# Opening stage of a hybrid encoder block: order of VectorE's work, sums of squares in pairs on GpSimd, row sums without a split

## The chip, the cores and the metric

The kernel runs on one core of a Trainium2 chip. A core has five engines that run side by side, each with its own queue, in order: TensorE (matmuls, into PSUM), VectorE, ScalarE, GpSimd and SyncE, which issues most DMAs. The profile calls them PE (and PEld for the loading of weights), DVE, ACT, POOL and SP. They share the on-chip memory SBUF and wait for each other through semaphores. The metric is the device time of one execution in microseconds (us); lower is better.

## The reference

The block takes 1024 positions of width 1024, puts 16 learned meta tokens in front (1040 positions), normalizes, projects into ten parts, runs a bidirectional retention and a windowed attention on them, merges, projects and normalizes again. What matters here is the start: the norm, the projection, and q, k and v of retention head 0.

```python
def _rms_norm(x, w):
    xf = x.astype(jnp.float32)
    y = xf * lax.rsqrt(jnp.mean(xf * xf, axis=-1, keepdims=True) + EPS)
    return (y * w.astype(jnp.float32)).astype(x.dtype)

def _hybrid_layer(h, pre_w, w_in, dec_f, dec_b, ...):
    u = _rms_norm(h, pre_w)
    z = u @ w_in
    rq, rk, rv, rg, aq, ak, av, ag, gr, ga = _split_in(z)
    rq = _pad_front(_rotary(rq.reshape(B, T, RET_HEADS, RET_DK), pos))
    rk = _pad_front(_rotary(rk.reshape(B, T, RET_HEADS, RET_DK), pos) * (RET_DK ** -0.5))
    rv = _pad_front(rv.reshape(B, T, RET_HEADS, RET_DV).astype(jnp.float32))
    lg_f = jax.nn.log_sigmoid(dec_f.astype(jnp.float32))
    lg_b = jax.nn.log_sigmoid(dec_b.astype(jnp.float32))
    o_r = _bidirectional_retention(rq, rk, rv, lg_f, lg_b)[:, META_PAD:]
    ...
```

The decays are powers of `exp(lg)`. The norm's factor of a row is a scalar, so the kernel projects `x * w` first and applies the factor later.

## The kernel before

**Precision.** Every operand of a large product is split into a high part (rounded to the fast matmul type, `R` in the code) and a low part (the rest), and a product is three matmuls: high times high (L74), then the two mixed ones (L75, L76). High parts are made by ScalarE or GpSimd, low parts by VectorE (`dve_lo`, L90, a subtraction; for x L329, one instruction that scales and subtracts).

**The opening stage.** x lies transposed, in eight blocks `xr[k]` of 128 channels by 1040 positions, loaded in order. For each block k:

- ScalarE makes the high part `xh[k]` (L327) and then the squares `sq[k]` (L348);
- VectorE makes the low part `xl[k]` (L329). In the trace both parts are called `big`;
- TensorE multiplies the block with the weights `w0` of q and k of head 0 into six PSUM banks (`qk0_mm`, L310; tiles `pq`, `pk`): first the products with the high part of x, last those with the low part (L76).

The weights w0 come in pieces; the low parts of the third piece (`third`, blocks 2 and 3) and of the last (`fifth`, blocks 4 to 7; in the trace `w<-wr`) are VectorE's too. Beside this stands a chain of small instructions on 8 columns, the decays: `exponentials`, `decays`, `decay_series` (nine steps that each need the one before), `decay_exponents`, and on GpSimd a power for the table `dtab` (`decay_columns`, L236).

The squares are summed block after block on VectorE (`add_square`, L321). The sum is then split, high on ScalarE (L361) and low on VectorE (`sql`), and TensorE multiplies both parts with a column of ones, 128 positions at a time, which gives the mean square of each row (`sums_by_rows`, L370, tile `pms`). These small products stand between those of the third V product.

**Behind the blocks** come: `pack_meta` (L151, the 16 meta columns of each block into `xm`); the weights of V, cast by ScalarE (L115, `wh`) and their low parts on VectorE (`wl`); three V products on TensorE (`projT`, tile `pv`): first that of the meta rows (L159, L161), then those of 128 rows each. The second and third need a PSUM bank that a piece of qk0 still holds. `evac_qk0(i)` frees it: VectorE rotates piece i by three multiplications from PSUM (L184 to L186, tile `m_qk`) and GpSimd adds two of the results (L187).

**What sets the order.** Each engine runs its queue in order. The queue is fixed when the program is built: a scheduler places the instructions by its estimate of when each can run, and `issue_after(i)` holds an instruction behind instruction i. Before the change the holds put on VectorE: low part 2, the whole decay chain up to the exponents, the first add of squares, and only then low part 3; from block 4 on the low part of block k stands behind the add of sums[k - 2]; and all adds but the last split stand before the first rotation.

## Time and profile before

| What | Value |
|---|---|
| Median of 3 runs | 1075.31 us (1073.83 to 1077.41) |
| The profiled execution | 1075.24 us |
| Its span, first to last instruction | 1073.5 us |
| Busy share: PE, PEld | 98%, 84% |
| Busy share: DVE, ACT, POOL | 81%, 45%, 20% |

A row of a timeline has start, duration, engine, source line, operation, tiles (written `<-` read), shapes, a count where equal rows are merged (the duration is then that of all), and in brackets how long the engine was idle before it and what ended that. A row of the waits has who waited for whom, us in total, how many times, and the longest. A row of groups has busy time, mean ns of one, and the idle time before. Source lines that name a helper stand for all its callers, so L90 is any low part but that of x, and L187 any add of a rotation.

### The profile page before, as it was taken

Reading aid. Unit: us, or ns where it says so; the run is one execution under the profiler, and the core shown is the slowest. Engines: PE = TensorE matmul, PEld = TensorE weight load, DVE = VectorE, ACT = ScalarE, POOL = GpSimd, SP = SyncE. Lnnn points to the kernel's source line nnn. Section 1 sums busy time; section 2 is a strip of 40 time slices with the busy share of each in tenths; the row PEclk is TensorE's granted clock in tenths of the full one; section 3 lists DMA queues with packets and bytes.
Section 4 is the critical chain, followed back from the end, with each engine's and each line's share of the span. In section 5 each row is a group of like instructions: output and inputs, shape, how many; then the busy total and the mean of one; then the engine's idle time right before and its main releaser. Section 6 shows DMA issues by size and latency. Waiting matters only on the chain.

```text
span 1073.5 us, 17195 instructions
## 1 busy us (share of the span) xinstructions
PE 1049.6 (98%) x5863; PEld 905.7 (84%) x5863; DVE 867.9 (81%) x1770; ACT 487.0 (45%) x1064; POOL 217.2 (20%) x270
## 2 busy tenths in 40 slices
PE   8999999999999999989999999999999999999997
PEld 7898999989989788878888888888888888787886
DVE  7897788768986677787668988999799799767765
ACT  7141442422413444456557545555456546333432
POOL 3234225133352333342210000000000000110032
PEclk9999999999999999999999999999999999999999
DMA  7121111203131455576758769899934746789464
GB/s 285 40 70 43 57 41 60 84 28 102 51 108 49 140 178 178 166 241 223 220 169 272 265 232 313 275 360 345 377 129 157 241 172 221 234 206 326 122 118 78
DMA packets 109304, 187.14 MB, mean 174 GB/s; under 512 B 10864, under 2 KB 49648, under 8 KB 108400
## 3 DMA queue, kind: packets, MB, share of 16 engines
q1 hardware_dynamic: 105328, 179.47, 50.5%
q0 software_dynamic: 3456, 6.29, 3.9%
q8 instruction: 46, 0.75, 0.3%
q10 hardware_dynamic: 432, 0.28, 0.1%
q14 instruction: 42, 0.34, 0.1%
HBM read 124.92 MB, written 61.87 MB: 174 GB/s over the span
## 4 chain that ended last, share of the span: by engine, by line
PE 86%; DVE 6%; DMA 3%; issue 2%; ACT 2%; POOL 1%; SPq 0%; DVEq 0%; POOLq 0%; ACTq 0%
PE bz L75 8%; PE bz L74 8%; PE bz L76 8%; PE pv L74 3%; PE pv L75 3%; PE pv L76 3%; PE paq L75 3%; PE paq L76 3%; PE paq L74 3%; PE br L75 2%; PE br L74 2%; PE br L76 2%; PE bo L75 2%; PE bo L74 2%; PE bo L76 2%; PE ba L75 2%
## 5 line engine op out<-in xcount | busy, mean ns | idle before, releaser
L1210 POOL DMA_DIRECT2D mx_d<-c1a x4 | 3.7, 918 | 396.2 <-DVE c1a L1201 396.2
L75 PE MATMUL bz<-T,llz 128*128 128x512 f32 x192 | 75.7, 394 | 0.0
L76 PE MATMUL bz<-T,lhz 128*128 128x512 f32 x192 | 75.6, 395 | 0.0
L74 PE MATMUL bz<-T,lhz 128*128 128x512 f32 x192 | 75.4, 394 | 0.0
L74 PE MATMUL pv<-wh,big 128*128 128x256 f32 x256 | 73.2, 286 | 1.3 <-DVE m_qk L186 1.3
L75 PE MATMUL pv<-wh,big 128*128 128x256 f32 x256 | 73.2, 286 | 0.0
L76 PE MATMUL pv<-wl,big 128*128 128x256 f32 x256 | 72.5, 283 | 0.0
L75 PE MATMUL bz<-big,llz 128*128 128x512 f32 x176 | 69.7, 396 | 0.0
L76 PE MATMUL bz<-big,lhz 128*128 128x512 f32 x176 | 69.3, 394 | 0.0
L74 PE MATMUL bz<-big,lhz 128*128 128x512 f32 x176 | 68.6, 394 | 0.0
L1379 POOL TENSOR_SCALAR p<-p,den 128x352 f32<-128x352 f32 (+2 forms) x60 | 44.6, 757 | 92.7 <-DVE den L1372 88.4
L1369 ACT ACTIVATE p<-raw,nm 128x353 f32<-128x353 f32 (+2 forms) x64 | 36.0, 565 | 47.7 <-DVE nm L1366 46.8
L74 PE MATMUL paq<-big,wh 128*128 128x512 f32 x128 | 51.4, 402 | 0.0
L75 PE MATMUL paq<-big,wl 128*128 128x512 f32 x128 | 50.6, 396 | 0.0
L76 PE MATMUL paq<-big,wh 128*128 128x512 f32 x128 | 50.5, 394 | 0.0
L74 PEld LDWEIGHTS pv<-wh,big 128*128 128x128 f32 x256 | 48.3, 189 | 1.7 <-DVE m_qk L186 1.6
L75 PEld LDWEIGHTS pv<-wh,big 128*128 128x128 f32 x256 | 48.3, 189 | 0.2
L76 PEld LDWEIGHTS pv<-wl,big 128*128 128x128 f32 x256 | 48.3, 189 | 0.0
L1366 DVE CUSTOM_DVE_ANT_0 raw<-ps,mask,nsink 128x352 f32<-128x352 f32 (+2 forms) x64 | 33.4, 553 | 16.1 <-PE ps L76 15.8
L75 PEld LDWEIGHTS bz<-T,llz 128*128 128x128 f32 x192 | 36.2, 188 | 8.5
L74 PEld LDWEIGHTS bz<-T,lhz 128*128 128x128 f32 x192 | 36.2, 188 | 8.4
L76 PEld LDWEIGHTS bz<-T,lhz 128*128 128x128 f32 x192 | 36.2, 188 | 8.4
(620 smaller groups left out, 3574.4 us busy)
## 6 DMA issues: line engine op xcount, KB each, us to landing
wrz<-in_w_in_dram SPq DMA_DIRECT2D x32, 512.0 KB, 5.7
wr<-in_w_in_dram SPq DMA_DIRECT2D x31, 512.0 KB, 4.0
e<-e SPq DMA_DIRECT2D x40, 256.0 KB, 4.5
we<-in_w_in_dram SPq DMA_DIRECT2D x16, 512.0 KB, 5.2
tg<-tg_d SPq DMA_DIRECT2D x32, 256.0 KB, 5.1
T<-preT SPq DMA_DIRECT2D x6, 1024.0 KB, 7.1
oTr_d<-ost SPq DMA_DIRECT2D x16, 256.0 KB, 2.1
aq_d<-aq SPq DMA_DIRECT2D x16, 256.0 KB, 2.2
```

The costliest lines, as they stand in the source:

```text
L74: nc.tensor.matmul(o, ah, bh, start=first, stop=False, **kw)
L75: nc.tensor.matmul(o, al, bh, start=False, stop=False, **kw)
L76: latest[:] = [nc.tensor.matmul(o, ah, bl, start=False, stop=last, **kw).ins]
L1210: nc.gpsimd.dma_start(d, to, accum_op=ALU.add)
L1366: nc.vector.tensor_tensor_reduce(raw[e_][:, 1:1 + wid], s[:, 0:wid], mask[:, mo:mo + wid], -SCALE, nsink[:, hp:hp + 1], ALU.add, ALU.min, ...
L1369: last["exp"] = nc.scalar.activation(p[:, 0:1 + wid], raw[e_][:, 0:1 + wid], AF.Exp, scale=-1.0, bias=nm_[:, e_:e_ + 1], accum_out=den[:, ...
L1379: nc.gpsimd.tensor_scalar(pt[e_][:, 0:wid], pt[e_][:, 0:wid], den[:, e_:e_ + 1], 1.0, op0=ALU.mult, op1=ALU.mult)
```

## The change

It concerns the opening alone:

- VectorE makes each block's low part before other work for that block; the decay chain is cut into pieces that stand behind the low parts of blocks 2 to 5.
- Squares are added in pairs (0 and 1, 2 and 3, 4 and 5, 6 and 7) on GpSimd; VectorE adds the four pair sums with three adds, one before block 6, one behind V's low parts, one behind the first rotation.
- The row sums take the sum of squares as plain float32: no split, one product in place of two.
- The low parts of V's weights are held behind the packing of the meta rows, one after the other (`"apart"` returns them for that), and six buffers for squares replace four.

```diff
@@ -115,9 +115,11 @@
                 nc.scalar.copy(h, t)
             else:
                 pool_hi(h, t)
-            dve_lo(l, t, h)
             hi.append(h)
             lo.append(l)
+            if act == "apart":
+                return lambda: dve_lo(l, t, h)
+            dve_lo(l, t, h)
 
         return split, ((lambda k, a, b: hi[k // 4][:, k % 4, a:b]), (lambda k, a, b: lo[k // 4][:, k % 4, a:b]))
 
@@ -192,7 +194,7 @@
     tabt = ra.tile([P, MW], F32, tag="tab", bufs=1, name="tabt")
     idx = tabt[:, 3 * P:3 * P + 5]
     warm = ra.tile([P, 1], F32, name="warm")
-    ones, onef = (ra.tile([P, 2], t, name=n) for n, t in (("ones", R), ("onef", F32)))
+    onef = ra.tile([P, 2], F32, name="onef")
     dect, neg, na, e, e2, s_, ss, acc, lg = (ra.tile([P, 8], F32, name=n) for n in (
         "dect", "neg", "na", "e", "e2", "s_", "ss", "acc", "lg"))
     ecst, ex = (ra.tile([P, 28], F32, name=n) for n in ("ecst", "ex"))
@@ -217,12 +219,13 @@
         v.tensor_tensor(ss, s_, s_, ALU.mult)
         v.tensor_scalar(acc, ss, 1.0 / 17, None, op0=ALU.mult)
 
-    def decay_series():
+    def decay_series(first, last):
         v = nc.vector
-        for j in (15, 13, 11, 9, 7, 5, 3):
-            v.scalar_tensor_tensor(acc, acc, 1.0 / j, ss, op0=ALU.add, op1=ALU.mult)
-        v.scalar_tensor_tensor(acc, acc, 1.0, s_, op0=ALU.add, op1=ALU.mult)
-        v.scalar_tensor_tensor(lg, acc, -2.0, lg, op0=ALU.mult, op1=ALU.add)
+        for j in (15, 13, 11, 9, 7, 5, 3, 1)[first:last]:
+            v.scalar_tensor_tensor(acc, acc, 1.0 / j, ss if j > 1 else s_, op0=ALU.add, op1=ALU.mult)
+
+    def decay_log():
+        nc.vector.scalar_tensor_tensor(lg, acc, -2.0, lg, op0=ALU.mult, op1=ALU.add)
 
     def decay_exponents():
         v = nc.vector
@@ -313,61 +316,68 @@
                     k == 0, k == KT - 1)
 
         nc.vector.memset(onef, 1.0)
-        nc.vector.tensor_copy(ones, onef)
         nc.vector.memset(ms, 1.0)
-        low, squares, sums = None, [], {}
-
-        def add_square(k):
-            sums[k] = nc.vector.tensor_tensor(squares[k], squares[k - 1], squares[k], ALU.add).ins
+        squares, at = [], [None]
+
+        def then(f):
+            with follow(*[x for x in at if x is not None]):
+                r = f()
+            if r is not None:
+                at[:] = [r if hasattr(r, "name") else r.ins]
+
+        def low(k, a, b):
+            return nc.vector.scalar_tensor_tensor(xl[k][:, a:b], xr[k][:, a:b], vec[:, k:k + 1],
+                                                  xh[k][:, a:b].bitcast(F32), op0=ALU.mult, op1=ALU.subtract)
+
+        def add_squares(e, i, k):
+            return e.tensor_tensor(squares[k], squares[i], squares[k], ALU.add)
 
         for k in range(KT):
             t = xr[k]
-            parts = [(0, 528), (528, T)] if k == 0 else [(0, T)]
-            for a, b in parts:
+            for a, b in [(0, 528), (528, T)] if k == 0 else [(0, T)]:
                 nc.scalar.activation(xh[k][:, a:b], t[:, a:b], AF.Copy, scale=vec[:, k:k + 1])
-                with tc.issue_after(sums[k - 2] if k > 3 else exponents) if k > 2 else ExitStack():
-                    low = nc.vector.scalar_tensor_tensor(xl[k][:, a:b], t[:, a:b], vec[:, k:k + 1],
-                                                         xh[k][:, a:b].bitcast(F32), op0=ALU.mult, op1=ALU.subtract)
+                then(lambda: low(k, a, b))
+            if k == 0:
+                with tc.issue_after(raised[1]):
+                    then(exponentials)
+                nc.gpsimd.tensor_tensor(e, ecst[:, 0:8], na, ALU.pow)
+            if k == 1:
+                then(third)
             if k == 2:
-                with tc.issue_after(low.ins):
-                    decays()
-                    decay_series()
-                    exponents = decay_exponents()
+                then(decays)
+            if k == 3:
+                then(lambda: decay_series(0, 3))
+                then(fifth)
+            if k == 4:
+                then(lambda: decay_series(3, 6))
+            if k == 5:
+                then(lambda: decay_series(6, 8))
+                then(decay_log)
+                then(decay_exponents)
+            qk0_mm(k)
+            squares.append(st.tile([P, T], F32, tag="sq", bufs=6, name=f"sq{k}"))
+            nc.scalar.activation(squares[k], t, AF.Square)
+            if k % 2:
+                add_squares(nc.gpsimd, k - 1, k)
+            if k == 5:
                 decay_columns()
-            if k == 0:
-                with tc.issue_after(low.ins), tc.issue_after(raised[1]):
-                    exponentials()
-                    nc.gpsimd.tensor_tensor(e, ecst[:, 0:8], na, ALU.pow)
-            if k == 1:
-                third()
-            if k == 3:
-                with tc.issue_after(exponents):
-                    fifth()
-            qk0_mm(k)
-            squares.append(st.tile([P, T], F32, tag="sq", bufs=4, name=f"sq{k}"))
-            nc.scalar.activation(squares[k], t, AF.Square)
-            if k > 1:
-                with tc.issue_after(exponents if k == 2 else low.ins):
-                    add_square(k - 1)
-        with tc.issue_after(low.ins):
-            pack_meta()
-            wv0 = load_w(w_in, U_V, act=True)
-
-        add_square(KT - 1)
-        with tc.issue_after(sums[KT - 1]):
-            rotated = evac_qk0(0)
-        sq = squares[-1]
-        sqh, sql = (st.tile([P, T], R, name=n) for n in ("sqh", "sql"))
-        nc.scalar.copy(sqh, sq)
-        with tc.issue_after(rotated):
-            split = dve_lo(sql, sq, sqh)
+                then(lambda: add_squares(nc.vector, 1, 3))
+        raw_v = fetch_w(w_in, U_V)
+        split_v, wv0 = halves_w(U_V)
+        then(pack_meta)
+        for t in raw_v:
+            then(split_v(t, "apart"))
+        then(lambda: add_squares(nc.vector, 3, 5))
+        rotated = evac_qk0(0)
+        at[:] = [rotated]
+        then(lambda: add_squares(nc.vector, 5, 7))
+        split, sq = at[0], squares[-1]
         pms = p1("pms")
 
         def sums_by_rows(k):
             for c in (k, 8)[:1 + k // 7]:
                 a, b = cols(c)
-                for i, t in enumerate((sqh, sql)):
-                    nc.tensor.matmul(pms[0:b - a, 2 * c:2 * c + 2], t[:, a:b], ones, start=i == 0, stop=i == 1)
+                nc.tensor.matmul(pms[0:b - a, 2 * c:2 * c + 2], sq[:, a:b], onef, start=True, stop=True)
 
         with tc.issue_after(split):
             rotated = evac_qk0(1)
```

ScalarE now takes each block's squares right behind its high part and casts V's weights last; TensorE's products of blocks 4 to 7 interleave a little differently; SyncE's queue is the same, and behind the opening all queues are the same as before. Three places in the queues follow; a row is line, operation, tiles (with numbers of the program's own), shape and, where rows are merged, a count.

GpSimd (POOL) from the high part of the third piece of w0 (`w0_0_0`) to the first adds of a rotation (`kr0`, `qr0`), before:

```order
L87 TENSOR_SCALAR w0_0_0_154<-wr0_0_153 128x512
L236 TENSOR_TENSOR dtab_103<-ecst_135,ex_136 128x28
L187 TENSOR_TENSOR kr0_429<-m1_qk0_0_430,m2_qk0_0_431 128x272
L187 TENSOR_TENSOR kr0_429<-m1_qk0_1_441,m2_qk0_1_442 128x256
L187 TENSOR_TENSOR qr0_4_536<-m1_qk0_4_537,m2_qk0_4_538 128x512
```

and now:

```order
L87 TENSOR_SCALAR w0_0_0_153<-wr0_0_152 128x512
L333 TENSOR_TENSOR sq1_251<-sq0_228,sq1_251 128x1040
L333 TENSOR_TENSOR sq3_305<-sq2_279,sq3_305 128x1040
L333 TENSOR_TENSOR sq5_359<-sq4_331,sq5_359 128x1040
L239 TENSOR_TENSOR dtab_103<-ecst_134,ex_135 128x28
L333 TENSOR_TENSOR sq7_406<-sq6_384,sq7_406 128x1040
L189 TENSOR_TENSOR kr0_426<-m1_qk0_0_427,m2_qk0_0_428 128x272
```

Three adds of squares now stand between the weight's high part and the power for dtab, and one between that and the first rotation.

VectorE (DVE) from the end of the decay chain to the low part of block 5 (`xr5`) before; `big` with `xr` is a low part of x, `w0_1_1` the low part of the last piece of w0:

```order
L229 TENSOR_TENSOR ex_136<-lg_134,tabt_122 128x16
L232 TENSOR_SCALAR ex_136<-lg_134,tabt_122 128x4
L233 TENSOR_SCALAR ex_136<-lg_134 128x8
L321 TENSOR_TENSOR sq1_253<-sq0_230,sq1_253 128x1040
L329 SCALAR_TENSOR_TENSOR big0_1_111<-xr3_148,vec_100,big0_0_109 128x1040
L90 TENSOR_TENSOR w0_1_1_158<-wr0_1_156,w0_1_0_157 128x1024
L321 TENSOR_TENSOR sq2_293<-sq1_253,sq2_293 128x1040
L329 SCALAR_TENSOR_TENSOR big1_1_112<-xr4_149,vec_100,big1_0_110 128x1040
L321 TENSOR_TENSOR sq3_317<-sq2_293,sq3_317 128x1040
L329 SCALAR_TENSOR_TENSOR big1_1_112<-xr5_150,vec_100,big1_0_110 128x1040
```

and now, from the last of the decay steps that stand behind block 2 to the first behind block 5:

```order
L219 TENSOR_TENSOR ss_131<-s__130 128x8
L329 SCALAR_TENSOR_TENSOR big0_1_111<-xr3_147,vec_100,big0_0_109 128x1040
L220 TENSOR_SCALAR acc_132<-ss_131 128x8
L225 SCALAR_TENSOR_TENSOR acc_132<-acc_132,ss_131 128x8 x2
L90 TENSOR_TENSOR w0_1_1_157<-wr0_1_155,w0_1_0_156 128x1024
L225 SCALAR_TENSOR_TENSOR acc_132<-acc_132,ss_131 128x8
L329 SCALAR_TENSOR_TENSOR big1_1_112<-xr4_148,vec_100,big1_0_110 128x1040
L225 SCALAR_TENSOR_TENSOR acc_132<-acc_132,ss_131 128x8 x3
L329 SCALAR_TENSOR_TENSOR big1_1_112<-xr5_149,vec_100,big1_0_110 128x1040
L225 SCALAR_TENSOR_TENSOR acc_132<-acc_132,ss_131 128x8
```

The adds of squares are gone from between the low parts, and steps of the series stand there.

VectorE around the low parts of V's weights (`wl4`) and the first rotation (`m1_qk0_0`, `m2_qk0_0`), before:

```order
L90 TENSOR_TENSOR wl4_0_421<-wr4_0_416,wh4_0_420 128x1024
L90 TENSOR_TENSOR wl4_1_425<-wr4_1_417,wh4_1_424 128x1024
L321 TENSOR_TENSOR sq6_386<-sq5_363,sq6_386 128x1040
L151 CAST xm_113<-big1_1_112 128x4x16
L321 TENSOR_TENSOR sq7_409<-sq6_386,sq7_409 128x1040
L184 TENSOR_TENSOR m1_qk0_0_430<-pk0_0_194,cr_119 128x272
L185 TENSOR_TENSOR m2_qk0_0_431<-pk0_0_194,sr_120 64x272
L186 TENSOR_TENSOR m2_qk0_0_431<-pk0_0_194,sr_120 64x272
L164 TENSOR_TENSOR vmeta0_447<-pv0_0_448,vmeta0_447 16x256
```

and now:

```order
L153 CAST xm_113<-big1_1_112 128x4x16
L90 TENSOR_TENSOR wl4_0_418<-wr4_0_409,wh4_0_417 128x1024
L90 TENSOR_TENSOR wl4_1_422<-wr4_1_410,wh4_1_421 128x1024
L333 TENSOR_TENSOR sq5_359<-sq3_305,sq5_359 128x1040
L186 TENSOR_TENSOR m1_qk0_0_427<-pk0_0_193,cr_119 128x272
L187 TENSOR_TENSOR m2_qk0_0_428<-pk0_0_193,sr_120 64x272
L188 TENSOR_TENSOR m2_qk0_0_428<-pk0_0_193,sr_120 64x272
L333 TENSOR_TENSOR sq7_406<-sq5_359,sq7_406 128x1040
```

One add of squares stands ahead of the rotation instead of two, and one behind it; the sum of the meta rows (`vmeta0`) has moved further back.

## The prediction

> **What bounds the kernel now.** I read the table of busy shares first (TensorE 98%, VectorE 81%), then TensorE's waits over the whole span, to see where the missing 2% lies.
>
> ```profile
> engine line waited for: us in total, times, longest us
> ...
> PE pt L1390 <- DVE pal L90: 2.3, 1, 2.3
> PE pq L76 <- DVE big L329: 2.0, 2, 1.6
> ...
> PE pv L74 <- DVE m_qk L186: 1.3, 1, 1.3
> PE pv L159 <- DVE xm L151: 0.9, 1, 0.9
> ```
>
> Three of these four are in the opening: L329 makes the low part of an x block, L151 packs the meta rows, L186 ends the first rotation. Together 2.0 + 1.3 + 0.9 = 4.2 us, and each releaser is VectorE. Next the opening by stages (length, then busy time of PE, PEld, DVE, ACT, POOL).
>
> ```profile
> 17.30:36.50 19.20, 15.00 (x96) 12.80 (x94) 19.10 (x26) 10.26 (x11) 5.20 (x1) 1.00 0.47 167
> 36.50:45.00 8.50, 8.48 (x73) 8.46 (x74) 5.80 (x12) 1.23 (x4) 3.77 (x5) 1.00 0.02 5
> ```
>
> From 17.3 to 36.5 VectorE is full (19.10 of 19.20) and TensorE has 4.2 us of holes; from 36.5 on TensorE is full. So one place decides: the start of the second V product at 36.52, which waits for a bank that the rotation of qk0 piece 0 frees.
>
> ```profile
> 36.02 0.44 DVE L186 TENSOR_TENSOR m_qk<-pk,sr 64x272 f32<-64x272 f32 x1
> 36.52 0.39 PE L74 MATMUL pv<-wh,big 128*128 128x256 f32 x1 [1.29 <-DVE m_qk L186]
> ```
>
> VectorE ends that rotation at 36.46 and TensorE starts 0.06 later. Behind it both programs have the same order on TensorE except the row sums, and no wait that a DMA ends is in the list, so whatever moves 36.52 moves the end by as much. The profiled execution took 1075.24 us, 1.74 over its span of 1073.5; the median of the runs shown is 1075.31, 0.07 above.
>
> **The change part by part.** *Fewer adds on VectorE.* Its queue had seven adds of squares ahead of the rotation; it keeps two there (sq3 += sq1, sq5 += sq3) and one behind it.
>
> ```profile
> L321 DVE TENSOR_TENSOR sq<-sq,sq 128x1040 f32<-128x1040 f32 x7 | 8.6, 1234 | 0.0
> 16.59 1.23 DVE L321 TENSOR_TENSOR sq<-sq,sq 128x1040 f32<-128x1040 f32 x1
> 17.74 1.29 DVE L329 SCALAR_TENSOR_TENSOR big<-xr,vec,big 128x1040 fp32r<-128x1040 f32 x1
> ```
>
> An add holds the queue for 17.74 - 16.59 = 1.15 us, so five fewer give 5.75 us. The decay series keeps its instructions, now between the low parts; low part 3 no longer stands behind 13 of them and an add, which is the 1.6 us hole.
>
> *Four adds on GpSimd.* The trace has no add of 1040 columns there; the nearest are the rotation's adds.
>
> ```profile
> L187 POOL TENSOR_TENSOR qr<-m_qk,m_qk 128x512 f32<-128x512 f32 x2 | 2.6, 1282 | 3.8 <-DVE m_qk L186 3.8
> L187 POOL TENSOR_TENSOR kr<-m_qk,m_qk 128x256 f32<-128x256 f32 x3 | 2.3, 750 | 5.4 <-DVE m_qk L186 5.4
> ```
>
> (1282 - 750) / 256 = 2.08 ns a column, so 1282 + 528 x 2.08 = 2.38 us each. Were they beside VectorE's work they would cost nothing. The trace says they are not beside it:
>
> ```profile
> 240.78 0.40 POOL L87 TENSOR_SCALAR Shb<-Sb 128x256 fp32r<-128x256 f32 x1
> 241.15 1.04 POOL L87 TENSOR_SCALAR wh<-wr 128x1024 fp32r<-128x1024 f32 x1
> 241.21 1.25 DVE L90 TENSOR_TENSOR Slb<-Sb,Shb 128x256 fp32r<-128x256 f32 x1 [0.89 <-POOL Shb L87]
> 447.75 1.47 POOL L187 TENSOR_TENSOR aq<-m_aq,m_aq 128x512 f32<-128x512 f32 x1 [3.38 <-issue]
> 447.99 2.31 DVE L90 TENSOR_TENSOR wl<-wr,wh 128x1024 fp32r<-128x1024 f32 x1
> 67.53 1.21 DVE L90 TENSOR_TENSOR wl<-wr,wh 128x1024 fp32r<-128x1024 f32 x1
> 67.60 1.40 POOL L87 TENSOR_SCALAR Shf<-Sf 128x256 fp32r<-128x256 f32 x1 [1.84 <-DVE klf L502]
> 69.40 0.41 DVE L90 TENSOR_TENSOR Slf<-Sf,Shf 128x256 fp32r<-128x256 f32 x1
> ```
>
> A VectorE subtraction of 256 columns takes 0.41; that at 241.21 took 1.25 and ended at 242.46, 0.27 after GpSimd's 241.15 + 1.04. One of 1024 columns takes 1.21; that at 447.99 took 2.31 and ended 1.08 after GpSimd's add. Both ended later than GpSimd by just their own columns (1.05 ns each): they did no work until GpSimd was done. At 67.60 it is the other way: GpSimd's copy, 0.40 alone, began in effect at 69.00 - 0.40 = 68.60, which is 0.14 before the recorded end of VectorE's subtraction. So instructions of the two engines take turns, whole, when VectorE reads two tiles from SBUF. In this opening nearly all do: low parts, weight low parts, adds, the series.
>
> The Trainium skill ("SBUF — State Buffer", section "Who interferes with whom") has this as an exclusive lock on a port pair against any GpSimd instruction that reads SBUF, held for the whole instruction. There the trace disagrees in one place, the power for dtab:
>
> ```profile
> 16.76 5.74 POOL L236 TENSOR_TENSOR dtab<-ecst,ex 128x28 f32<-128x28 f32 x1 [5.41 <-DVE ex L233]
> ```
>
> VectorE's low part at 17.74 ran its usual 1.29 within it. By the page taken literally the power, now among the adds, would add up to 5.7 us; by the row nothing, and I count nothing.
>
> *The turns, one by one.* ScalarE sets when each add can start:
>
> ```profile
> 14.11 1.06 ACT L348 ACTIVATE sq<-xr 128x1040 f32<-128x1040 f32 x1
> 16.00 3.27 ACT L327 ACTIVATE big<-xr,vec 128x1040 fp32r<-128x1040 f32 x3
> 10.35 1.00 POOL L87 TENSOR_SCALAR w<-wr 128x512 fp32r<-128x512 f32 x1
> 11.38 0.69 DVE L90 TENSOR_TENSOR w<-wr,w 128x512 fp32r<-128x512 f32 x1 [0.51 <-POOL w L87]
> 12.22 1.30 DVE L329 SCALAR_TENSOR_TENSOR big<-xr,vec,big 128x1040 fp32r<-128x1040 f32 x1
> ```
>
> First: sq1 is long ready when GpSimd ends its weight copy at 11.35, so its add starts at once (as at 240.78 + 0.40 and 241.15), ahead of VectorE's 11.38. It ends near 13.70, the weight's low part at 13.70 + 0.54 = 14.24 instead of 12.07. VectorE stood until 12.22 then anyway, so low part 2 starts 1.95 later, at 14.17.
> Second: sq3 is ready at 15.17; the add takes over 0.14 before low part 2 ends (15.47), so 15.33 to 17.71. The first small decay instruction ends at 17.73 instead of 15.60: +2.15.
> Third: ScalarE now alternates high parts and squares from 16.00 (1.06 and 0.96 apart), sq5 is ready at 20.14. The weight's low part (20.2 to 21.4) goes first, the add 21.25 to 23.63, and the next decay step is 2.15 late. If the add wins there, the weight pays the same.
> Fourth: the exponents end near 27.8, the power 33.6, the add follows V's second low part (34.56): 34.4 to 36.8. VectorE's sq5 += sq3 is queued just there, and with it the rotation: +2.2.
> Sum on VectorE's queue: 1.95 + 2.15 + 2.15 + 2.2 = 8.45, less 5.75: **+2.7 us**. The rotation ends at 39.16, the V product starts at 39.2. TensorE is done with its earlier work before that:
>
> ```profile
> 22.59 0.73 PE L76 MATMUL pq<-big,w 128*128 128x512 f32 x2 [0.39 <-DVE big L329]
> ...
> 34.95 0.28 PE L161 MATMUL pv<-wl,xm 128*16 128x256 f32 x1
> ```
>
> From the low products of block 4 to the end of the first V product it is 22.59 to 35.07, less 1.0 of waiting for the meta rows: 11.4 us. Block 4's low products now wait from 22.7 for low part 4, until 25.0; behind that the low parts lead. 25.0 + 11.4 = 36.4, so VectorE sets the end.
>
> *Bounds.* An add of 2.3 to 2.5 us gives +2.4 to +3.2; small operations not held back, -0.4; if adds stretch to 2.6, +3.6. If no turns were taken, the loss is zero and the gain is TensorE's holes, 4.2 us, at most about 5 with the restart of each.
>
> *Costed at nothing.* Row sums in plain float32: nine products for eighteen, but the only plain product in the trace, L493, shows as two passes each:
>
> ```profile
> 50.73 0.39 PE L493 MATMUL tr<-qr,kr 128*128 128x128 f32 x2
> 40.32 0.17 PE L370 MATMUL pms<-ones,sqh 128*128 128x2 f32 x1
> 40.35 0.25 PE L370 MATMUL pms<-ones,sql 128*128 128x2 f32 x1
> ```
>
> So eighteen passes either way; bounds: 9 x 0.11 saved or, if slower, lost, 1 us. The split of the sum (sql, 1.57 on VectorE; sqh on ScalarE) falls away behind 36.5, where VectorE has 2.7 us to spare: nothing. The meta-row add moves behind a third rotation, to about 44; its reader on TensorE comes 7.6 after 39.2. SP's fetch of V's second half waits for the weight's low part, 1.2 later; ScalarE casts it some 4 us after. The dtab power ends 11 us later than before, 15 before its reader. If any of these covers went, it would cost its own overrun, tenths.
>
> **The rivals.**
> *Adds run beside VectorE (faster).* If two long reads share better than the quoted rows, VectorE finishes the rotation near 30.7 and TensorE's 4.2 to 5 us of holes close: 1070.6. For it: the power did run beside VectorE. Against: that reads 28 columns, the add at 447.75 reads 512 of two tiles, as ours do. It decides once an add costs VectorE less than 5.75 / 4 = 1.4 us.
> *VectorE keeps its turn.* If its back-to-back stream shut GpSimd out, only the first and last adds would bite: 4.15 - 5.75, near 1074. Against it: at 67.60 GpSimd got in at the next boundary.
> *TensorE's clock falls back.* The new waits are longer than those in the opening now, and further on the trace shows what a long one can do:
>
> ```profile
> 463.26 0.63 PE L1390 MATMUL pt<-ident,p 128*128 128x128 f32 x4 [2.31 <-DVE pal L90]
> ...
> 464.64 0.29 PE L76 MATMUL pak<-big,wh 128*128 128x256 f32 x1
> 464.76 0.39 PE L74 MATMUL pak<-big,wh 128*128 128x256 f32 x1
> ...
> 465.16 0.42 PE L76 MATMUL pak<-big,wh 128*128 128x256 f32 x1
> 465.38 0.42 PE L74 MATMUL pak<-big,wh 128*128 128x256 f32 x1
> ...
> 468.15 0.31 PE L75 MATMUL pak<-big,wl 128*128 128x256 f32 x1
> 468.30 0.28 PE L76 MATMUL pak<-big,wh 128*128 128x256 f32 x1
> ```
>
> Matmuls of 256 columns start 0.12 apart until 464.76, then 0.21 to 0.22 apart until 468.15, though the granted clock reads 1.00: 3.4 us at about half speed after a wait of 2.31, so 1.7 us lost. The new opening has two such waits: 2.3 us in block 4, up to 25.0, and 2.8 us ahead of 39.2. A relapse after the first costs nothing, since TensorE would be done at 36.4 + 1.7 = 38.1, still before VectorE, and the last wait shrinks to 1.1. A relapse after the last one falls where TensorE is full and costs its 1.7: 1079.7. Against it: the first wait probably takes it. It decides if the first wait does not and the last does.
> The Trainium skill ("TensorE: Matmul & The Clock Gate", section "Why this matters for your kernels") sets the bound for such a fall at idle gaps of about 3 us. By that neither wait would do it and this rival would go; the trace shows it after 2.31, and the measurement decides.
>
> **How the numbers follow.** Turns as summed: 1075.24 + 2.7 = 1077.9, 0.07 more against the median: **1078.0 us**, chance 0.65, its own range 1076.5 to 1079.5. Beside VectorE 0.11 (1070.6); VectorE keeps its turn 0.07 (1074); clock 0.17 (1079.7). About 0.3%, 3.2 us, is what a measurement can tell from no change: 1072.1 and 1078.5. The sum lies just inside, and what I left out (restarts of TensorE, longer adds) adds time, so I give the first case 0.32 above that line and 0.33 below. Slower: 0.32 + 0.17 = 0.49; same: 0.33 + 0.07 = 0.40; faster 0.11. The range 1074 to 1081 leaves out the faster case and a tail.
>
> **What would show it.** Right: four GpSimd adds of 2.3 to 2.5 us (longer where they wait); beside each a VectorE instruction, some of eight columns, of over 2 us; a wait of TensorE near 3 us for the first rotation, and the V product at 39.2. Wrong: VectorE instructions of usual length beside the adds and that product near 31.5; or GpSimd's adds of 3.5 us and VectorE unhurt. Matmuls of 256 columns 0.21 apart behind 39.2 would be the clock.

## The result, and the profile after

The changed kernel took 1079.68 us (median of 12, 1076.40 to 1080.68) against 1075.40 us (median of 12) for the kernel before in the same comparison: 1.0036 of it, 95% interval 1.0021 to 1.0050. It is slower by 4.3 us. Two later comparisons of the unaltered changed kernel gave 1.0047 (1.0032 to 1.0063) and 1.0038 (1.0023 to 1.0053). The profiled execution took 1080.68 us, its span is 1078.5 (before: 1075.24 and 1073.5).

First GpSimd's queue in the opening, from the timeline of the changed kernel. L333 is now the add of two squares, on either engine; L239 is the dtab power.

```profile
11.70 2.41 POOL L333 TENSOR_TENSOR sq<-sq,sq 128x1040 f32<-128x1040 f32 x1
14.98 3.21 POOL L333 TENSOR_TENSOR sq<-sq,sq 128x1040 f32<-128x1040 f32 x1 [0.87 <-ACT sq L359]
19.96 2.46 POOL L333 TENSOR_TENSOR sq<-sq,sq 128x1040 f32<-128x1040 f32 x1 [1.76 <-ACT sq L359]
27.95 5.74 POOL L239 TENSOR_TENSOR dtab<-ecst,ex 128x28 f32<-128x28 f32 x1 [5.54 <-DVE ex L236]
33.67 3.24 POOL L333 TENSOR_TENSOR sq<-sq,sq 128x1040 f32<-128x1040 f32 x1
```

Then what VectorE did at those moments, from the same timeline:

```profile
11.76 2.89 DVE L90 TENSOR_TENSOR w<-wr,w 128x512 fp32r<-128x512 f32 x1 [0.51 <-POOL w L87]
...
15.79 2.43 DVE L216 TENSOR_SCALAR e<-e 128x8 f32<-128x8 f32 x1
...
19.99 2.46 DVE L220 TENSOR_SCALAR acc<-ss 128x8 f32<-128x8 f32 x1
...
28.94 2.50 DVE L329 SCALAR_TENSOR_TENSOR big<-xr,vec,big 128x1040 fp32r<-128x1040 f32 x2
...
34.55 3.46 DVE L333 TENSOR_TENSOR sq<-sq,sq 128x1040 f32<-128x1040 f32 x1
...
38.82 0.44 DVE L188 TENSOR_TENSOR m_qk<-pk,sr 64x272 f32<-64x272 f32 x1
```

Beside each add stands one stretched VectorE instruction: 2.89 us where that subtraction took 0.69 before, 2.43 and 2.46 for instructions of eight columns, 3.46 for an add of 1.23. The two low parts inside the dtab power took 2.50 together, 1.25 each, as always. Two of the four stretched rows, L216 and L220, read one SBUF tile and not two. The second and fourth GpSimd add show 3.2 us because GpSimd in turn stood until VectorE was done. The rotation ends at 39.26 instead of 36.46.

What TensorE waited for in the opening, and two later marks (`tr` is the first transposition of k, 46.81 in the kernel before):

```profile
14.71 0.50 PE L75 MATMUL pq<-big,w 128*128 128x512 f32 x1 [1.32 <-DVE w L90]
...
20.13 0.73 PE L76 MATMUL pq<-big,w 128*128 128x512 f32 x2 [0.69 <-DVE big L329]
...
24.04 0.73 PE L75 MATMUL pq<-big,w 128*128 128x512 f32 x2 [1.87 <-DVE w L90]
...
39.32 0.39 PE L74 MATMUL pv<-wh,big 128*128 128x256 f32 x1 [0.86 <-DVE m_qk L188]
...
49.83 0.27 PE L501 MATMUL tr<-ident,kr 128*16 128x128 f32 x1
```

The second V product starts at 39.32 instead of 36.52 (+2.80), the transposition stands 3.02 later. The last wait is only 0.86 because TensorE itself was late. The view by stretches (length, busy time of PE with its count, then the granted clock, the DMA share and GB/s) shows why:

```profile
25.08:28.98 3.90, 3.90 (x14) 0.56 0.36 127
28.98:36.00 7.02, 7.02 (x47) 1.00 0.20 68
```

Behind the wait in block 4 the clock was at about half for 3.4 us, and then full. So the opening explains 3.0 of the 5.0 us by which this span is longer. Most of the rest is one more such stretch, at 271 us, where both kernels have the same work (the last section comes back to it). TensorE's wait just ahead of it ends 2.91 us later than before (268.82 for 265.91), its next long one 4.35 later (467.61 for 463.26).

### The profile page after: what moved, and what is told of

Same layout as the page of the kernel before. It is cut to its first block, busy times and chain, and to the rows that moved or that the text cites. A ratio compares the mean times of both kernels' runs of the same rounds, so it can differ in the third digit from the quotient of the medians.

```text
span 1078.5 us, 17188 instructions
## 1 busy us (share of the span) xinstructions
PE 1052.0 (98%) x5863; PEld 907.7 (84%) x5863; DVE 870.3 (81%) x1764; ACT 486.4 (45%) x1063; POOL 229.9 (21%) x274
## 4 chain that ended last, share of the span: by engine, by line
PE 84%; DVE 7%; DMA 4%; issue 2%; ACT 1%; POOL 1%; SPq 0%; DVEq 0%; POOLq 0%; ACTq 0%
PE bz L74 7%; PE bz L75 7%; PE bz L76 7%; PE pv L74 3%; PE pv L75 3%; PE pv L76 3%; PE br L75 2%; PE br L74 2%; PE br L76 2%; PE paq L75 2%; PE paq L76 2%; PE bo L75 2%; PE paq L74 2%; PE bo L74 2%; PE bo L76 2%
## 5 line engine op out<-in xcount | busy, mean ns | idle before, releaser
L74 PEld LDWEIGHTS pv<-wh,big 128*128 128x128 f32 x256 | 48.9, 191 | 1.2 <-DVE m_qk L188 1.2
```

What stands on the lines that cost most here:

```text
L74: nc.tensor.matmul(o, ah, bh, start=first, stop=False, **kw)
```

## The experiments

All changes are to the changed kernel unless said otherwise. Medians and ratios are against the kernel before in the same comparison. "Product" is the start of the second V product, "tr" that of the first transposition of k, both in the profiled execution.

| Run | Product | tr | Median | Before | Ratio (95%) |
|---|---|---|---|---|---|
| kernel before | 36.52 | 46.81 | | | |
| changed kernel | 39.32 | 49.83 | 1079.68 | 1075.40 | 1.0036 (1.0021 to 1.0050) |
| e1_no_pair_adds | 31.41 | 41.78 | 1071.25 | 1076.38 | 0.9955 (0.9939 to 0.9971) |
| e2_pair_adds_on_vector | 34.93 | 45.40 | 1073.66 | 1076.38 | 0.9974 (0.9961 to 0.9987) |
| e3_plain_sums_alone | 36.81 | 47.26 | 1076.90 | 1076.38 | 1.0005 (0.9993 to 1.0017) |
| e5_one_tile_read | 33.98 | 44.47 | 1073.64 | 1076.38 | 0.9976 (0.9964 to 0.9989) |
| e6_adds_behind_rotation | 31.26 | 42.35 | 1073.91 | 1076.64 | 0.9984 (0.9971 to 0.9998) |
| e7_change_again | 39.03 | 51.05 | 1081.02 | 1076.64 | 1.0047 (1.0032 to 1.0063) |
| e8_last_add_behind | 35.13 | 45.60 | 1076.11 | 1076.64 | 0.9999 (0.9988 to 1.0010) |
| e9_five_ahead | 33.93 | 44.48 | 1073.43 | 1075.58 | 0.9983 (0.9969 to 0.9996) |
| e10_filled_wait | 39.15 | 49.61 | 1079.31 | 1075.58 | 1.0033 (1.0019 to 1.0048) |
| e12_change_beside_filled | 39.43 | 51.46 | 1079.83 | 1076.25 | 1.0038 (1.0023 to 1.0053) |
| e13_filled_wait_again | 39.36 | 49.76 | 1078.24 | 1076.25 | 1.0024 (1.0010 to 1.0038) |
| e14_four_behind | 32.07 | 44.76 | 1074.22 | 1076.25 | 0.9987 (0.9971 to 1.0002) |

### Are GpSimd's adds the loss? (e1)

```diff
-            if k % 2:
-                add_squares(nc.gpsimd, k - 1, k)
```

> The changed kernel without GpSimd's four pair adds; nothing takes their place, so the even blocks' squares are left out of the row sums. Turns theory (each add held one VectorE instruction for a whole add): the four held instructions return to their usual 0.69, 0.16, 0.15 and 1.23 us, VectorE ends the first rotation near 30.3, TensorE becomes the bound and the second V product starts at 32.3 to 33.5 instead of 39.32; time 1071 to 1072.5, 0.996 to 0.997 of before. Rival, adds free and the new order of VectorE's queue itself the loss: the product stays near 39 and the time near 1079.

From its timeline, VectorE's four instructions that had been stretched, the end of the rotation, and the product:

```profile
11.38 0.69 DVE L90 TENSOR_TENSOR w<-wr,w 128x512 fp32r<-128x512 f32 x1 [0.51 <-POOL w L87]
...
13.25 0.17 DVE L216 TENSOR_SCALAR e<-e 128x8 f32<-128x8 f32 x1
...
15.27 0.17 DVE L220 TENSOR_SCALAR acc<-ss 128x8 f32<-128x8 f32 x1
...
27.91 1.24 DVE L333 TENSOR_TENSOR sq<-sq,sq 128x1040 f32<-128x1040 f32 x1
...
29.96 0.44 DVE L188 TENSOR_TENSOR m_qk<-pk,sr 64x272 f32<-64x272 f32 x1
...
31.41 0.28 PE L74 MATMUL pv<-wh,big 128*128 128x256 f32 x1
```

All are back at their usual lengths. The rotation ends at 30.40, 8.86 us earlier than with the adds, and TensorE starts the product at 31.41 without a wait. (The openings of two profiles are shifted by some tenths: the third weight piece's low part starts at 11.38 here and in the kernel before, at 11.76 in the changed kernel. Counted from there the adds cost 8.5.) The time falls 5.1 us under before. So the loss goes with the adds, and none is left for the order around them.

### On VectorE instead (e2)

```diff
             if k % 2:
-                add_squares(nc.gpsimd, k - 1, k)
+                then(lambda: add_squares(nc.vector, k - 1, k))
```

> The changed kernel with the four pair adds on VectorE, 1.15 us each, in place of GpSimd's. Turns theory: 4.6 us of adds in place of some 9.0 us of holding, so the first rotation ends near 34.9 and the second V product starts at 34.9 to 35.5; time 1073.5 to 1074.5, 0.998 to 0.999 of before. Rival, that GpSimd's adds did run beside VectorE and saved work: 4.6 us more on VectorE than in the changed kernel, product near 44, time 1083.

```profile
34.43 0.44 DVE L188 TENSOR_TENSOR m_qk<-pk,sr 64x272 f32<-64x272 f32 x1
...
34.93 0.39 PE L74 MATMUL pv<-wh,big 128*128 128x256 f32 x1
```

The rotation ends at 34.87, as the turns theory has it, and the ratio of 0.9974 is a little better than its 0.998 to 0.999. The same four adds cost less on the full engine (34.87 against e1's 30.40, 4.5 us) than on the idle one (8.9, or 8.5 from the third weight piece on). This version beats both kernels.

### What makes VectorE stand: one tile read or two? (e5)

GpSimd's add becomes a product with 1.0 in place; all queues keep their order.

```diff
             if k % 2:
-                add_squares(nc.gpsimd, k - 1, k)
+                nc.gpsimd.tensor_scalar(squares[k], squares[k], 1.0, 1.0, op0=ALU.mult, op1=ALU.mult)
```

> The changed kernel with each of GpSimd's four adds replaced by a product of one square tile with 1.0 in place (128x1040, one tile read in place of two, same place in every queue); the even blocks' squares are left out of the row sums. If only an instruction that reads two tiles holds VectorE: GpSimd's instructions take about 2.0 us by its 128x512 one of 1.0, VectorE keeps its usual lengths beside them, the second V product starts at 32.3 to 33.5 and the time is 1071 to 1072.5. If any streaming GpSimd instruction holds it: VectorE instructions of 1.7 us and more stand beside them, four times some 1.8 us, the product starts near 37.5 and the time is near 1077.

Three of the four places in its timeline, GpSimd's row and VectorE's:

```profile
11.93 1.08 POOL L361 TENSOR_SCALAR sq<-sq 128x1040 f32<-128x1040 f32 x1
11.99 1.55 DVE L90 TENSOR_TENSOR w<-wr,w 128x512 fp32r<-128x512 f32 x1 [0.52 <-POOL w L87]
...
15.22 1.07 POOL L361 TENSOR_SCALAR sq<-sq 128x1040 f32<-128x1040 f32 x1 [2.21 <-ACT sq L359]
15.31 0.99 DVE L219 TENSOR_TENSOR ss<-s__130 128x8 f32<-128x8 f32 x1
...
29.71 1.88 POOL L361 TENSOR_SCALAR sq<-sq 128x1040 f32<-128x1040 f32 x1
30.58 2.10 DVE L333 TENSOR_TENSOR sq<-sq,sq 128x1040 f32<-128x1040 f32 x1
```

Neither branch had its number right, since the instruction takes 1.08 us and not 2.0. But the question is decided: a GpSimd instruction that reads one tile makes VectorE stand too. The subtraction at 11.99 ends at 13.54, 0.53 behind GpSimd's 13.01, which is its own 512 columns; the eight columns at 15.31 end at 16.30, 0.01 behind GpSimd's 16.29. The hold shrinks with GpSimd's instruction: four times some 0.86 us, and counted from the third weight piece the rotation ends 2.9 us behind that of e1 instead of 8.5.

### The row sums alone (e3, from the kernel before)

```diff
-        sqh, sql = (st.tile([P, T], R, name=n) for n in ("sqh", "sql"))
-        nc.scalar.copy(sqh, sq)
-        with tc.issue_after(rotated):
-            split = dve_lo(sql, sq, sqh)
+        split = rotated
...
-                for i, t in enumerate((sqh, sql)):
-                    nc.tensor.matmul(pms[0:b - a, 2 * c:2 * c + 2], t[:, a:b], ones, start=i == 0, stop=i == 1)
+                nc.tensor.matmul(pms[0:b - a, 2 * c:2 * c + 2], sq[:, a:b], onef, start=True, stop=True)
```

> The kernel before with the row sums from plain float32 alone (no high and low part of the sum of squares). As predicted (eighteen passes either way): the second V product stays at 36.5, the fourth starts 7.6 to 7.8 us behind it, time within 0.3 us of before. Rival, that a plain float32 product costs more than two passes: the fourth starts 8.6 us behind and the time is 1 us longer.

The product stands at 36.81 and tr 10.45 behind it, where the kernel before has 10.29: 0.16 us more. The time can't be told from before.

### The old order with one add less ahead of the rotation (e8, from e3)

```diff
-        add_square(KT - 1)
-        with tc.issue_after(sums[KT - 1]):
+        with tc.issue_after(sums[KT - 2]):
             rotated = evac_qk0(0)
+        with tc.issue_after(rotated):
+            add_square(KT - 1)
...
-        split = rotated
+        split = sums[KT - 1]
```

> The kernel before with plain row sums and the last square add moved behind the first rotation; old order otherwise, so five adds wait in a row as before. If the queue ahead of the rotation is what counts, whatever its order: the rotation ends 1.15 earlier, the second V product starts near 35.4 and the time is 1.0 to 1.2 under before, ratio 0.999. Rival, that the gain of the kernel with all adds on VectorE (2.7 us) came from the new order alone: no gain here, product at 36.5.

The product starts at 35.13, 1.39 earlier than in the kernel before, and within 0.2 of e2, which has the new order. So the new order of low parts and decays by itself moved the product by little; what moved it in e2 is the add behind the rotation. In the time, 0.9999 (0.9988 to 1.0010), a gain of 1.2 us can't be seen, nor can it be excluded. Nor is it shown why e2, with product and tr within 0.2 of these, gains some 2 us more: of e2's 2.7 us the opening accounts for 1.4.

### Is 4.3 us the opening alone? (e7, e12: the changed kernel; e10, e13: its last wait filled)

> The changed kernel unaltered, to see how much of the first comparison's 4.3 us stays. If the opening's loss (2.8 us at the second V product and 0.2 from the row sums) is all: 3.0 us over before, ratio 1.002 to 1.0035, and a profile with fewer half-speed stretches of TensorE shows a span nearer to 1076. If something else is lost for good behind 47 us: 4.3 us and more again, ratio 1.004.

> The changed kernel once more, on the same chip as the one with the filled wait, since their two ratios so far (1.0047 and 1.0033) overlap. Opening alone: 3.0 us over before, ratio 1.0028. With half-speed stretches behind its last wait in a good part of the executions: 4 us and more, ratio 1.004, and a higher mean than the filled one.

In both profiles the wait in block 4 (1.86 and 1.85 us) left the clock alone, and TensorE's last row ended at 36.6 and 37.0, so the last wait was 2.44 us. From e12, the end of the meta rows' product, the second V product, and the clock in stretches:

```profile
36.70 0.28 PE L163 MATMUL pv<-wl,xm 128*16 128x256 f32 x1
39.43 0.39 PE L74 MATMUL pv<-wh,big 128*128 128x256 f32 x1 [2.44 <-DVE m_qk L188]
...
40.62 0.41 PE L74 MATMUL pv<-wh,big 128*128 128x256 f32 x1
40.83 0.42 PE L75 MATMUL pv<-wh,big 128*128 128x256 f32 x1
...
44.01 0.28 PE L75 MATMUL pv<-wh,big 128*128 128x256 f32 x1
44.13 0.28 PE L76 MATMUL pv<-wl,big 128*128 128x256 f32 x1
```

```profile
39.43:40.60 1.17, 1.17 (x9) 0.98 0.00 0
40.60:44.00 3.40, 3.40 (x18) 0.51 0.00 0
44.00:48.00 4.00, 4.00 (x37) 1.00 0.01 4
```

Matmuls of 256 columns stand 0.21 apart from 40.62 to 44.0, at a granted clock of 0.51, and 0.12 apart on either side. In e12 as in e7, tr stands 12.02 to 12.03 behind the product instead of 10.51: 1.5 us that nothing absorbs. The control fills the wait:

```diff
         if c == 0:
+            for _ in range(10 if name == "pv0_0" else 0):
+                nc.tensor.matmul(t[0:48, 0:256], xm[:, 0, 0:48], wh(0, 0, 256), start=True, stop=True,
+                                 skip_group_check=True)
             for k in range(KT):
```

> The changed kernel with ten matmuls more on TensorE (128x256, 0.117 us apart, 1.2 us in all; they write the bank of the meta rows' product, which starts afresh behind them), placed between TensorE's work on block 7 and that product; every other queue is the same. They only shorten the last wait. Clock theory (the wait of 2.4 us ahead of the second V product brings a half-speed stretch behind it in a part of the executions, 1.7 us each, and that is why the measured loss is 4.3 and not 3.0 us): no half-speed matmuls behind 39 us, the upper group of times goes, ratio to before 1.002 to 1.0035, though TensorE does more. Rival, that the rest of the loss has nothing to do with that wait: ratio 1.0045 or more, as the change had it.

> The changed kernel with the ten matmuls that shorten the last wait, once more. If that wait costs something through the clock on average: 0.7 to 1.5 us under the unaltered changed kernel of this call. If not: the same within 0.5 us.

The stretches of e10 behind block 4's wait and behind the product:

```profile
25.00:28.20 3.20, 3.20 (x11) 0.50 0.39 145
39.15:47.00 7.85, 7.85 (x69) 1.00 0.01 2
```

In both profiles the fall came in block 4, where it is absorbed, and none behind the product: tr stands 10.46 and 10.40 behind it. But so it was in the first profile of the changed kernel, with its wait unfilled, so these two profiles do not show what the filling does where block 4 lets the clock alone. What is left is the times. In the one comparison that held both, the mean of the filled kernel is 1.5 us lower (1078.48 of 12 executions, 1080.00 of 8). Over all comparisons the changed kernel's mean lies 4.1 us over before (3.96, 4.20 and 4.22 for 12, 6 and 8 executions), the filled one's 3.2 (3.79 and 2.70, 12 each). The granted clock of every execution is on record too: its mean is 0.9937 for these 26 executions, 0.9946 for the 24 of the filled kernel and 0.9948 for 100 of the kernel before. One stretch of 3.4 us at half clock is 0.0016 of a span, so the changed kernel has some 0.6 stretches more per execution than the filled one. All this points the way the clock theory says, but roughly: the ratios of the two kernels overlap, and that the upper times would go did not come true (e10 has times up to 1083.78).

### Trying to keep the gain (e6, e9, e14)

All three put low parts first, have the adds one after the other, and leave the plain row sums. They differ in how many adds stand behind the rotation.

```diff
-            if k % 2:
-                add_squares(nc.gpsimd, k - 1, k)
+            if k in (3, 4):
+                then(lambda: add_squares(nc.vector, k - 3, k - 2))
...
+        with tc.issue_after(joined[0]):
+            add_squares(nc.gpsimd, 6, 7)
...
+        then(lambda: add_squares(nc.vector, 3, 4))
+        then(lambda: add_squares(nc.vector, 4, 5))
+        then(lambda: add_squares(nc.vector, 5, 7))
```

> A version meant to keep what the change has that is good: low parts first, decay in pieces, plain row sums; three square adds on VectorE ahead of the first rotation (one after the other), the other four behind it: one on GpSimd beside VectorE's rotations, which read PSUM, three on VectorE behind the third rotation; the nine row-sum products stand together at the end of the third V product. Turns theory, with rotations not held: rotations keep 0.43 and 0.69 us beside a GpSimd add of 2.4, the first rotation ends near 31.6, the second V product starts there, the time is 4.5 to 5 us under before, ratio 0.995 to 0.996. If GpSimd's add holds the rotations too, or the sums come late for their products: TensorE waits 1 to 2 us ahead of the fourth V product, ratio 0.997.

From e6: GpSimd's add with VectorE's rotations beside it, then what came of the row sums (L382) and V's high parts (L504).

```profile
31.70 2.43 POOL L335 TENSOR_TENSOR sq<-sq,sq 128x1040 f32<-128x1040 f32 x1
31.79 0.43 DVE L190 TENSOR_TENSOR m_qk<-pk,sr 64x256 f32<-64x256 f32 x1
...
32.59 0.67 DVE L188 TENSOR_TENSOR m_qk<-pq,cr 128x512 f32<-128x512 f32 x1
...
39.78 0.40 ACT L504 CAST vh<-vmeta 16x256 fp32r<-16x256 f32 x1 [7.95 <-DVE sq L335]
39.87 2.08 PE L382 MATMUL pms<-onef,sq 128*16 128x2 f32 x18
...
43.83 0.58 PE L74 MATMUL pv<-wh,big 128*128 128x256 f32 x1 [1.11 <-DVE vl L90]
```

```profile
42.30:44.00 1.70, 0.54 (x2) 0.50 0.00 0
44.00:48.90 4.90, 4.90 (x23) 0.50 0.00 0
```

The rotations are not held: 0.43 and 0.67 us as ever beside an add of 2.43. TensorE reached the product at 31.26, 5.3 us earlier than before. Then most of it was given back: V's high parts waited until the last add (39.74), TensorE waited 1.11 us for their low parts, and from 42.3 to 48.9 it ran at half clock. Ratio 0.9984: the second branch by its wait, and less of a gain than its 0.997.

e9 leaves five adds ahead and two behind, all on VectorE; e14 three ahead, four between the second and the third rotation, with the nine products at the end of the third V product.

> As the version with four adds behind the rotation, but none on GpSimd: five square adds on VectorE ahead of the first rotation, one after the other, two behind the second rotation and ahead of the third; the row-sum products stand in the third V product again. No GpSimd instruction reads SBUF ahead of the rotation, so the first rotation ends at 30.9 + 2 x 1.15 = 33.2, the second V product starts there, the sums are ready 3.6 us later and nothing waits for them: 3.3 us under before, ratio 0.9965 to 0.9975. If the wait of some 2 us that TensorE then has ahead of the product brings a half-speed stretch in part of the executions: ratio 0.998.

> A version without GpSimd adds: low parts first, decay in pieces, three square adds on VectorE ahead of the first rotation and four between the second and the third, the row-sum products at the end of the third V product. The first rotation ends at 30.9, TensorE sets the start of the second V product at 31.3; the sums are ready near 37.3, ahead of their products at 39; no SBUF turn is given to GpSimd but for two of its rope adds. 4.5 us under before, ratio 0.9955 to 0.9965. If the third rotation or the high parts of V, which come later for the adds ahead of them, hold TensorE behind the third V product: 1 to 2 us of it are given back, ratio 0.9975.

e9 has its product at 33.93 behind a wait of 1.96 us and tr 2.3 us earlier than before; 0.9983 is about what that gives, though in its profile no half clock stood behind that wait. e14 missed both its branches. Its product stands at 32.07, but TensorE waited 0.71 us for the sums, and behind the products of two columns the clock fell again:

```profile
38.61:40.55 1.94, 1.94 (x19) 1.00 0.00 0
40.60:44.00 3.40, 3.40 (x17) 0.50 0.00 0
```

None of the three is better than e2 (0.9974).

## Why the prediction came out as it did

The time predicted was 1078.0 us in a range of 1074 to 1081; 1079.68 was measured. Place, mechanism and sign are as predicted. The time lies 0.2 above the range of the forecast itself (1076.5 to 1079.5) and on the number of the rival with the clock (1079.7). That agreement is in part luck: the twelve times stand in two groups, five up to 1078.1 and seven from 1079.3 on, and the median falls on the lower edge of the upper one. The mean is 1078.88, and the profiled execution, one of the slowest, had no fall of the clock behind the last wait.

- **GpSimd's add, estimated at 2.38 us.** Measured 2.41 and 2.46 where it did not stand itself. Right.
- **Whole turns, also for eight columns; 8.45 us in sum.** The four stretched rows are longer than usual by 2.20 + 2.27 + 2.30 + 2.23 = 9.0; by e1 it is 8.5 from the third weight piece on. Right. The condition "when VectorE reads two tiles from SBUF" is too narrow, though: L216 and L220 read one and stood as long. At the third add GpSimd won, and both the decay step and the weight's last low part were late; that was the variant named, at the same price.
- **Five adds fewer, 5.75 us.** e1's rotation ends at 30.40, 6.06 us before that of the kernel before (36.46). Right within the shifts.
- **The sum, +2.7, product at 39.2.** It stands at 39.32, 39.03 and 39.43 in three profiles of the changed kernel, at 36.52 in the kernel before and 36.81 in e3: +2.6 between the means. That whatever moves this start moves the end by as much held in e1 (5.1 us both), not in e6 and e14, where part was lost again behind it.
- **The dtab power counted at nothing.** Right: two low parts ran 1.25 us each within it. The Trainium skill ("SBUF — State Buffer", section "Who interferes with whom") lets a GpSimd instruction that reads SBUF hold the shared ports for its whole length; by that a low part here would have stood for up to 5.7 us, which the row at 28.94 excludes. For the adds and for e5's one-tile read, beside VectorE's two-tile reads, the section and the rows agree, as they do on the rotations of e6, which have one input in PSUM.
- **Plain row sums at nothing, bounds of 1 us.** Measured 0.2: tr stands 10.51 behind the product instead of 10.29, and 10.45 in e3.
- **TensorE done at 36.4, a wait near 3 us.** Without a fall of the clock its last row ended at 36.6 and 37.0 and it waited 2.44. With one in block 4 it ended at 38.5 and the wait was 0.86, near what the text had (38.1 and 1.1). The one wait of 2.3 us in block 4, for low part 4, was in fact 1.87 for the weight's last low part, and 1.32 more stood in block 2, which the text did not have.
- **The rivals that were faster.** Both fell: no add ran beside VectorE's two-tile reads, and VectorE kept no turn against an add that came first.
- **TensorE's clock, chance 0.17.** This is the step that was too weak: "the first wait probably takes it". In two of the three profiles of the changed kernel it did not, and the fall came behind the last wait at 1.5 us (1.7 was the price). With e10 and e13, whose work up to block 4 is the same, the first wait took it in three of five. By these shares the clock costs 0.6 to 1.0 us on average; with 2.6 and 0.2 from the opening that makes 3.4 to 3.8, beside 4.1 measured over 26 executions. The shares rest on five profiles, and the rest stays open. One reading in the text is wrong: behind the wait of 2.31 us the granted clock reads not 1.00 but 0.50, as the spacing of the matmuls says too:

```profile
464.76:468.15 3.39, 3.39 (x19) 0.50 0.49 155
```

Why the sign is negative at all: the pair adds were to use an engine that stood idle, but in this opening VectorE reads SBUF nearly all the time, mostly two tiles at once, and an add that takes 1.15 us in its queue makes it stand 2.2 us when GpSimd does it.

## What to carry to other kernels

Before work is moved from VectorE to GpSimd, look at what VectorE does at that moment. Beside its reads from SBUF each add of 1040 columns cost it the add's whole length, even where it handled eight columns; beside rotations that read PSUM the same add was free, and a power on 28 columns held none of the two-tile reads. Here it was cheaper to leave the work on the full engine; and an add moved behind the instruction that others wait for let TensorE start 1.0 to 1.4 us earlier (e9 against e2, e8 against the kernel before), which pays as long as nothing behind it comes late. And a wait of TensorE is to be priced with what may follow it, a stretch at half clock, since it depends on the execution whether that comes at a place where it is absorbed.

## What the runs showed of the hardware

**The raster of the clock.** Stretches of half clock stand in every profile but e8's, nearly all behind waits of 0.6 to 2.4 us (another at the very end, where TensorE runs out of work, is left aside). The changed kernel's later ones:

```profile
268.00:274.74 6.74, 5.99 (x31) 0.75 0.11 39
...
469.50:472.70 3.20, 3.20 (x17) 0.50 0.47 136
...
489.70:493.10 3.40, 3.40 (x17) 0.51 0.88 258
```

By the spacing of its matmuls they end at 28.98, 274.74, 472.76 and 493.15: 72.0, 58.0 and 6.0 times 3.413 us apart. e7's ends (43.6, 275.71, 473.74, 494.14) fit the same step, at another offset. So the clock changes on a raster, a fixed grid of times that lies differently in each execution, and a place can fall in one and not in the next.

The wait of 0.6 us that ends at 268.82 in the changed kernel, and in the same work of the others between 260 and 271, shows it. In eight profiles the clock fell behind it (the changed kernel's three, e5, e6, e9, e10, e13), and in these a step of the raster lies 1.8 to 2.6 us behind the wait's end. In the six where it did not (the kernel before, e1, e2, e3, e8, e14) the next step lies 0.05 to 1.6 us behind it. What goes with a fall is idle time within one step: of all the steps of the fourteen profiles between 12 and 1060 us, 26 have TensorE idle for 1.70 us or more, half of the step, and the clock fell at the end of every one. Of the other 4258 it did so at the end of 14, eight of them at this wait, with 0.75 us idle. That is how a wait of 1.87 us in block 4 is followed by a fall or not: in the changed kernel's first profile it lies within one step, in e7 and e12 it is cut in two.

This is where part of the spread of one kernel's times comes from, several us, as large as what is compared here: over the 100 executions of the kernel before with a clock on record, time and granted clock have a correlation of -0.62. e8's profile, without such a stretch, has a span of 1071.1 us. The Trainium skill ("TensorE: Matmul & The Clock Gate", section "What's actually happening") describes a free-running window of 3413 ns, which the ends above bear out; it puts the fall behind at least one idle window, while here half a window of idle time was enough.

**Narrow products may not keep the clock.** In e6 and e14 TensorE ran 18 passes of two columns for some 2 us, busy by the profile, and in both half clock began right behind (42.3 and 40.6). In e6 the step that ends there has only 0.21 us idle, in e14 0.71, the wait for the sums. In e9, with eight such passes in 0.96 us, it did not fall. Two cases, without a control.

**GpSimd stands as well.** The adds at 14.98 and 33.67 show 3.2 us for work of 2.4, and e5's product at 29.71 shows 1.88 for 1.08: the turn binds whichever engine comes second.
